# One state chain on one core: weight rows requested by ScalarE, stores and loads moved by half a pair, and the wide matrix work dealt out differently

## The chip, the core and the metric

The kernel runs on one core of one Trainium2 chip. The metric is the device time of one execution in microseconds (us). The engines are TensorE (PE; its weight loads are shown apart as PEld), VectorE (DVE), ScalarE (ACT), GpSimd (POOL) and SyncE (SP), which here only issues transfers. A letter q behind an engine (SPq, ACTq) means its queue of transfer requests, which is worked off in order: a request that has to wait for a semaphore holds up everything behind it on the same engine.

## The reference, cut to what matters

The reference is one layer of a decoder trunk on 1024 tokens of width 1024, in float32. The part around the change:

```
h = rms_norm(x);  z = h @ w_in            # pool, q, r/k/v + loras, 3 gates
y_pool = pool_branch(z_pool) @ w_proj_pool
y_mem  = mem_attention(z_q) @ w_proj_mem  # 4 heads, 256 memory tokens
# rwkv: 16 heads of 64, a state of 64x64 for each, step by step over the tokens
state = state * w_t + (state @ a_t) b_t^T + v_t k_t^T ;  y_t = state @ r_t
y_rwkv = (group_norm(y) + bonus) * g @ w_proj_rwkv
x = x + rms_norm((sum of the 3 gated branches) @ w_o);  then a ConvFFN
```

## The kernel before, in words

Every float32 weight row is split into a high and a low part, and each product of a wide matrix is made of three multiplications (high by high, high by low, low by high, lines 173 to 175). One weight block of the input projection (`in_block`, 128 output columns) has 8 k-steps for each of two halves of the tokens, so 16 k-steps or 48 multiplications of 128x512. Its weights come in four pieces of 128x256. For each piece `load_more` (line 159) requests the transfer into `wraw` on SP (line 163); `split_w` (line 129) then makes `whi` on ACT (line 131) and `wlo` on POOL (line 137). There are 3 buffers of `wraw` and 4 each of `whi` and `wlo`.

The state recurrence is done in chunks of 64 tokens. Four groups (`rwkv_group`, line 461, four heads each, g = 0 to 3) prepare it: gates and decays (`psu` products, line 488, then ACT), products of small matrices (`ps`, lines 586 and 593, and transposes `pt`, line 616), and a triangular solve that runs on DVE alone (31 steps, lines 639 and 641, then two transposes, lines 642 and 643). TensorE uses the solve's result in 32x32 products (`pz`, line 657, and `pw`, line 665). What a group made is spilled to memory.

Then one chain (`chain`, line 701) goes through 16 chunks, two to a pair. Each chunk is three visits of small products that depend on each other through copies on DVE and ACT: `pr`, then `py`/`pu` (with lines 764 and 773/774 behind them), then `ph`/`py` (with lines 790, 792 behind them). For each pair `load(b)` fetches `hv`, `ring`, `pair`, `bk` and `rb` (lines 718 to 722), one pair ahead. After a pair's second chunk `outputs` (line 680) loads two gate tiles `gt` (line 686), normalises the pair's output (a product `pvar`, line 693, and DVE operations, lines 695 to 698) and stores it as `d_y` (line 699).

Blocks that nobody waits for fill TensorE's time: 24 of the 32 blocks in the list `fill` (pool, query and gate columns, the results stored as `d_zp`, `d_zq`, `d_zg` by line 339) are dealt out by `fill_to(n)`, where n counts k-steps; the other 8 blocks stand in the attention that follows. `fill_to(n, behind)` makes the work wait in the scheduler's order behind a given instruction. Before the change n reaches 32, 48 and 64 behind the solves of groups 0, 1 and 2, then 96 and 160 in group 3; the chain asks for 172 at its first visit and 319 at its last, and the last 64 k-steps (to 384) stand behind the chain. The first thing behind them is the memory branch: loads of `mraw` (line 846), squares (line 850), a sum `pmm` (line 851), normalised halves `mh` and `ml`, and the key/value blocks. Its tiles lie in memory that the chain gives back.

The order on each engine is made by a scheduler from this program order, from data dependences, from buffer counts and from the extra order edges that `later` adds; those edges carry no semaphore.

Of the kernel before, what the change touches and what calls it, by code (L numbers as in the profile page):

```python
# [9 lines left out]
F32 = mybir.dt.float32  # L10
FR = mybir.dt.float32r
AF = mybir.ActivationFunctionType
ALU = mybir.AluOpType
# [4 lines left out]
P = 128  # L18
# [3 lines left out]
C = 64  # L22
# [22 lines left out]
def trunk_kernel(ctx: ExitStack, tc: tile.TileContext, xT, memT, pvec, w_in, w_kv, w_upd, w_upg,  # L45
                 w_pool, w_ppool, w_pmem, w_prwkv, w_o, w_fup, w_fdn, out):
    nc = tc.nc
    V, A, G, PE, SP = nc.vector, nc.scalar, nc.gpsimd, nc.tensor, nc.sync
# [15 lines left out]
    d_g = dtile([8, P, T], "d_g")  # L64
    d_bv = dtile([8, P, T], "d_bv")
# [4 lines left out]
    d_hv = dtile([NCH // 2, P, 4, 2, 2 * C], "d_hv")  # L70
    d_y = dtile([8, P, T], "d_y")
# [30 lines left out]
    for lo in (0, 64):  # L102
        s = slice(lo, lo + 64)
# [21 lines left out]
        return (lo_eng or V).tensor_tensor(lo, src, hi.bitcast(F32), op=ALU.subtract)  # L125

    hi_on_act, lo_on_dve, last_whi, hold = [False], [False], [None], [None]

    def split_w(src, hi, lo):
        if hi_on_act[0]:  # L130
            i = A.copy(hi, src)  # L131
            last_whi[0] = i.ins
            if hold[0] is not None:
                later(i, hold[0])
        else:
            G.tensor_scalar(hi, src, 1.0, 0.0, op0=ALU.mult, op1=ALU.add)
        (V if lo_on_dve[0] else G).tensor_tensor(lo, src, hi.bitcast(F32), op=ALU.subtract)  # L137
# [21 lines left out]
    def load_more(ps, ap, k0, n, kp):  # L159
        raw = wp.tile([P, kp, P], F32, name="wraw", tag=f"wraw{ps.c}", bufs=3)  # L160
        hi = wp.tile([P, kp, P], FR, name="whi", tag=f"whi{ps.c}", bufs=4)
        lo = wp.tile([P, kp, P], FR, name="wlo", tag=f"wlo{ps.c}", bufs=4)
        SP.dma_start(raw[:, :n], ap[:, k0:k0 + n])
        split_w(raw[:, :n], hi[:, :n], lo[:, :n])
        for j in range(n):
            ps.append((hi[:, j], lo[:, j]))
# [48 lines left out]
    def later(i, ins, plain=False):  # L215

        tc.add_manual_dep(i if plain else i.ins, ins.name, nosync, reason="order")
# [5 lines left out]
    rw = rw_ctx.enter_context(tc.tile_pool(name="rw", bufs=1))  # L223
# [7 lines left out]
    for k in range(KC):  # L231
        tag = ("X01", "X11", "HV", "HV")[k // 2]
# [228 lines left out]
    def rwkv_group(g, kv):  # L461
# [43 lines left out]
        for i in range(2):  # L505
            p = 2 * g + i
# [8 lines left out]
            for t0, _ in HALVES:  # L515
                s = slice(t0, t0 + 512)
# [124 lines left out]
            V.tensor_tensor(S[:, s + 1:, 0:m], S[:, s + 1:, 0:m], tm, op=ALU.add)  # L641
        V.transpose(S11.rearrange("p u s -> p s u"), S.rearrange("p t s -> p s t"))
        V.transpose(X.rearrange("p u t -> p t u"), S)
        if g == 3:
            fill_to(96)
        fill_to((32, 48, 64, 160)[g], solve if g == 3 else None)
        for us in (slice(0, NCH), slice(NCH, 2 * NCH)):
            for q, (qs, bs) in enumerate(quads):
                place = V.tensor_copy(NTu[qs, us, bs], X[qs, us]).ins
# [24 lines left out]
    def spill(dst, at_, src):  # L674
# [2 lines left out]
            dst = dst[:, :, n]  # L677
        SP.dma_start(dst.rearrange("c p t -> p c t"), src.rearrange("p (c u) s -> p c (u s)", u=2))

    def outputs(b, y, q):  # L680

        bt = slice(b * 2 * C, (b + 1) * 2 * C)
        gt = []
        for src, e in ((d_bv, "ld"), (d_g, "la")):
            gt.append(lr.tile([P, 8, 2 * C], F32, name="gt", tag=e))
            SP.dma_start(gt[-1], src[:, :, bt].rearrange("n p t -> p n t"))
        ln_w = pv[:, PV["ln_w"][0]:PV["ln_w"][0] + 8]
        for n in (0, 4):
            ns = slice(n, n + 4)
            y_, q_ = y[:, ns], q.rearrange("p (n t) -> p n t", t=2 * C)  # L690
            A.activation(q_, y_, AF.Square)
            ps = pss.tile([P, 512], F32, name="pvar", tag="s")
            PE.matmul(ps, bones, q, start=True, stop=True)
            rstd(q, ps, 2, 1.0 / 64)
            V.tensor_tensor(y_, y_, q_, op=ALU.mult)
            V.tensor_tensor(y_, y_, ln_w[:, ns].unsqueeze(2).broadcast_to([P, 4, 2 * C]), op=ALU.mult)
            V.tensor_tensor(y_, y_, gt[0][:, ns], op=ALU.add)
            V.tensor_tensor(y_, y_, gt[1][:, ns], op=ALU.mult)
        SP.dma_start(d_y[:, :, bt].rearrange("n p t -> p n t"), y)

    def chain(fills):

# [8 lines left out]
        def load(b):  # L711

            ar, nt = ring[:, b % 2], pair[:, b % 2, 0]
            hv = rw.tile([P, 8, 2, 2, C], F32, name="hv", tag=f"X{b % 2}2")
            rb = rw.tile([P, 8, 2, 2 * C], F32, name="rb", tag=f"X{b % 2}1")
            bk = rw.tile([P, 8, 2, P], F32, name="bk", tag=f"X{b % 2}0")
            for q, e in ((up, 0), (lo, 1)):
                SP.dma_start(hv[q, :, :, e], d_hv[b, q].rearrange("p g i (u s) -> p (g i) u s", u=2))
            SP.dma_start(ar, d_ar[b].rearrange("p g i e t -> p (g i) e t"))
            SP.dma_start(nt, d_nt[b].rearrange("p g i t -> p (g i) t"))  # L720
            SP.dma_start(bk, d_bk[b].rearrange("p g i u s -> p (g i) u s"))
            SP.dma_start(rb, d_rb[b].rearrange("p g i e t -> p (g i) e t"))
            held[b] = ar, nt, hv, rb, bk, pair[:, b % 2, 1]
# [25 lines left out]
        for c in range(NCH):  # L749
            b, u = divmod(c, 2)  # L750
            if u == 0 and 0 < b < NCH // 2 - 1:
                load(b + 1)
            ar, nt, hv, rb, bk, y = held[b]
            t = slice(u * C, (u + 1) * C)
            once = dict(start=True, stop=True)
            pr = bank("pr")
            py = pss.tile([P, 8, C], F32, name="py", tag="s")
            ke, ko = (up, lo) if c == 0 else (slice(0, P), slice(0, P))
            row = []
            for i in range(8):  # L760
                row.append(((pr[up, i], ar[ko, i, 2, t], hv[ko, i, u, 1]), once))
                row.append(((pr[lo, i], ar[ke, i, 0, t], hv[ke, i, u, 0]), once))
            visit(row, ready)
            made = V.tensor_copy(Rs, pr).ins
            pu = bank("pu")
            row = []
            for i in range(8 if c else 0):
                kw = dict(start=i == 0, stop=False)
                row.append(((py[lo, i], hv[lo, i, u, 0], ar[lo, i, 1, t]), kw))
                row.append(((py[up, i], hv[up, i, u, 1], ar[up, i, 1, t]), kw))  # L770
            row += [((pu[q, i], nt[q, i, t], Rs[q, i]), once) for i in range(8) for q in (lo, up)]
            visit(row, made)
            V.tensor_copy(hv[lo, :, u, 0], pu[lo])
            ready = A.copy(hv[up, :, u, 1], pu[up]).ins
            row = []
            if c + 1 < NCH:
                ph = bank("ph")
                for i in range(8):
                    row.append(((ph[up, i], bk[:, i, u, 64:128], hv[:, i, u, 1]), once))
                    row.append(((ph[lo, i], bk[:, i, u, 0:64], hv[:, i, u, 0]), once))  # L780
            for i in range(8):
                kw = dict(start=c == 0 and i == 0, stop=i == 7)
                row.append(((py[lo, i], hv[:, i, u, 0], rb[:, i, 0, t]), kw))
                row.append(((py[up, i], hv[:, i, u, 1], rb[:, i, 1, t]), kw))
            visit(row, ready)
            if c + 1 < NCH:
                hx = held[(c + 1) // 2][2]
                for q, e in ((lo, 0), (up, 1)):
                    if c == 0:
                        ready = V.tensor_copy(hx[q, :, 1 - u, e], ph[q]).ins  # L790
                    else:
                        ready = V.tensor_tensor(hx[q, :, 1 - u, e], ph[q], Hd[q], op=ALU.add).ins
                if c + 2 < NCH:
                    if c == 0:
                        V.tensor_copy(Hn, ph)
                    else:
                        V.tensor_tensor(Hn, ph, Hd, op=ALU.add)
                    for i in range(8):
                        A.activation(Hd[:, i], Hn[:, i], AF.Identity, scale=Dc[:, i, c + 1:c + 2])
            A.copy(y[:, :, t], py)  # L800
            if u:
                outputs(b, y, root)

    fill = [(j, spilled(d_zp[j])) for j in range(4)] + [(4 + j, spilled(d_zq[j])) for j in range(4)]
    fill += [(34 + j, spilled(d_zg[j], col("gate_b", j))) for j in range(24)]
# [2 lines left out]
    def fill_to(n, behind=None):  # L808

        while len(filled) < n:  # L810
            j, ev = fill.pop(0)
            in_block(j, ev, 1, filled, behind)
        return filled[n - 1]
# [6 lines left out]
    hi_on_act[0] = True  # L820
    for g in range(4):
        kv = rwkv_group(g, kv)
    chain(lambda v: 172 + 148 * v // 47)
    fill_to(384)
    rw_ctx.close()
    lr_ctx.close()

# [945 lines left out]
```

## Time and profile before

| | |
|---|---|
| median of 3 runs | 2033.92 us (2033.43 to 2038.42) |
| the profiled execution, its own time | 2039.66 us |
| its span, first to last instruction | 2037.9 us |
| mean granted TensorE clock | 0.976 |
| solves and `pz` products of groups 0 to 3 | `pz` starts at 226.3, 360.2, 508.1 and 643.2 us |
| chain | first `pr` at 672.4 us, last `pvar` at 907.9 us |
| memory branch and attention | first `pmm` at 944.1 us, last `po` at 1089.7 us |

Rows of groups read: line, engine, operation, out<-in, shape, count, busy time, mean ns of one, idle time before them and what ended it. A row of the timeline reads: start, duration, engine, line, operation, out<-in, count, and in brackets how long the engine had been idle before it and what released it. A row of waits reads: who waited for whom, total us, times, longest us. A row of windows reads: the stretch, its length, then busy time and count of PE, PEld, DVE, ACT and POOL, the mean granted TensorE clock (1.00 is full), the busy share of the transfer engines and GB/s.

### The profile page before, as it was taken

Reading aid. Unit: us, or ns where it says so; the run is one execution under the profiler, and the core shown is the slowest. Engines: PE = TensorE matmul, PEld = TensorE weight load, DVE = VectorE, ACT = ScalarE, POOL = GpSimd, SP = SyncE. Lnnn points to the kernel's source line nnn. Section 1 sums busy time; section 2 is a strip of 40 time slices with the busy share of each in tenths; the row PEclk is TensorE's granted clock in tenths of the full one; section 3 lists DMA queues with packets and bytes.
Section 4 is the critical chain, followed back from the end, with each engine's and each line's share of the span. In section 5 each row is a group of like instructions: output and inputs, shape, how many; then the busy total and the mean of one; then the engine's idle time right before and its main releaser. Section 6 shows DMA issues by size and latency. Waiting matters only on the chain.

```text
span 2037.9 us, 33739 instructions
## 1 busy us (share of the span) xinstructions
PE 1950.6 (96%) x12218; PEld 1574.1 (77%) x12218; DVE 1346.7 (66%) x2015; ACT 1048.9 (51%) x2158; POOL 779.2 (38%) x867
## 2 busy tenths in 40 slices
PE   7999998998988989899999999999999999999997
PEld 5777776776777767678788888887878888888886
DVE  8677669649664234443763453668889888877698
ACT  6675574753752334444555334546545544545544
POOL 4422213203201110112222345555579888832441
PEclk9999999979988999999999999999999999999999
DMA  4325244243276679845324544545322222269776
GB/s 153 127 80 164 84 141 123 71 130 101 85 223 218 203 237 263 226 139 173 105 81 158 189 134 128 181 146 174 109 91 88 78 88 83 83 214 244 166 184 148
DMA packets 284998, 296.25 MB, mean 145 GB/s; under 512 B 34720, under 2 KB 235552, under 8 KB 281760
## 3 DMA queue, kind: packets, MB, share of 16 engines
q1 hardware_dynamic: 271904, 278.90, 44.6%
q0 software_dynamic: 11856, 14.16, 4.3%
q8 instruction: 96, 1.57, 0.3%
q10 hardware_dynamic: 1072, 1.05, 0.2%
q14 instruction: 70, 0.57, 0.1%
HBM read 207.00 MB, written 87.03 MB: 144 GB/s over the span
## 4 chain that ended last, share of the span: by engine, by line
PE 49%; DVE 1%; DMA 1%; issue 0%; ACT 0%; POOL 0%; SPq 0%; ACTq 0%; DVEq 0%; POOLq 0%
PE psg L175 7%; PE psg L173 7%; PE psg L174 7%; PE psf L175 5%; PE psf L173 5%; PE psf L174 5%; PE psd L174 3%; PE psd L175 3%; PE psd L173 3%; PE ptr L964 0%; DMA d_f<-ug 0%; PE psn L1239 0%; PE po L173 0%; DMA wraw<-in_w_fup 0%; DMA kvr<-in_w_kv 0%
## 5 line engine op out<-in xcount | busy, mean ns | idle before, releaser
L137 POOL TENSOR_TENSOR wlo<-wraw,whi 128x256 fp32r<-128x256 f32 x464 | 398.1, 870 | 961.6 <-ACT whi L131 912.4
L173 PE MATMUL psg<-hh,whi 128*128 128x512 f32 x928 | 379.4, 409 | 32.2 <-ACT whi L131 25.6
L175 PE MATMUL psg<-hh,wlo 128*128 128x512 f32 x928 | 372.7, 402 | 2.6 <-POOL wlo L137 2.4
L174 PE MATMUL psg<-hl,whi 128*128 128x512 f32 x928 | 374.5, 404 | 0.7 <-DVE hl L259 0.6
L131 ACT CAST whi<-wraw 128x256 fp32r<-128x256 f32 x472 | 180.8, 403 | 245.7 <-PE psg L174 89.9
L173 PEld LDWEIGHTS psg<-hh,whi 128*128 128x128 f32 x928 | 178.2, 192 | 76.9 <-ACT whi L131 27.5
L175 PEld LDWEIGHTS psg<-hh,wlo 128*128 128x128 f32 x928 | 177.8, 192 | 44.8 <-POOL wlo L137 6.9
L174 PEld LDWEIGHTS psg<-hl,whi 128*128 128x128 f32 x928 | 178.3, 192 | 40.6 <-issue 2.5
L1099 POOL TENSOR_TENSOR wt<-a,wt 128x256 fp32r<-128x256 f32 x136 | 156.6, 1175 | 36.2 <-ACT wt L1098 36.1
L174 PE MATMUL psd<-f,u 128*128 128x512 f32 x292 | 113.8, 390 | 0.2 <-DVE f L1515 0.2
L175 PE MATMUL psd<-f,u 128*128 128x512 f32 x292 | 113.7, 389 | 0.0
L173 PE MATMUL psd<-f,u 128*128 128x512 f32 x292 | 113.2, 391 | 0.0
L175 PE MATMUL psf<-h2h,wt 128*128 128x512 f32 x272 | 106.0, 390 | 0.9 <-POOL wt L1099 0.9
L173 PE MATMUL psf<-h2h,wt 128*128 128x512 f32 x272 | 106.0, 390 | 0.3 <-ACT wt L1098 0.3
L174 PE MATMUL psf<-h2l,wt 128*128 128x512 f32 x272 | 105.9, 389 | 0.0
L1113 DVE SCALAR_TENSOR_TENSOR d<-z,pv,d 128x1023 f32<-128x1023 f32 x68 | 100.4, 1479 | 2.3
L1099 POOL TENSOR_TENSOR wt<-s,wt 128x256 fp32r<-128x256 f32 x68 | 79.6, 1190 | 3.7 <-ACT wt L1098 2.9
L173 PE MATMUL psf<-t,wt 128*128 128x512 f32 x204 | 79.4, 389 | 0.0
L175 PE MATMUL psf<-t,wt 128*128 128x512 f32 x204 | 79.4, 389 | 0.0
L174 PE MATMUL psf<-t,wt 128*128 128x512 f32 x204 | 79.4, 389 | 0.0
L1111 ACT ACTIVATE d<-z,pv 128x1024 f32<-128x1024 f32 x34 | 42.4, 1247 | 66.2 <-DVE z L1193 50.5
L1098 ACT CAST wt<-a 128x256 fp32r<-128x256 f32 x136 | 50.7, 404 | 42.2 <-POOL wt L1099 23.4
(430 smaller groups left out, 4605.5 us busy)
## 6 DMA issues: line engine op xcount, KB each, us to landing
wraw<-in_w_in SPq DMA_DIRECT2D x232, 128.0 KB, 2.5
a<-in_w_fup SPq DMA_DIRECT2D x128, 128.0 KB, 2.4
d_ar<-AR SPq DMA_DIRECT2D x24, 512.0 KB, 3.4
ring<-d_ar SPq DMA_DIRECT2D x8, 1536.0 KB, 7.2
d_zg<-st SPq DMA_DIRECT2D x48, 256.0 KB, 2.8
wraw<-in_w_fup SPq DMA_DIRECT2D x80, 128.0 KB, 2.5
fraw<-d_f SPq DMA_DIRECT2D x33, 256.0 KB, 3.9
d_rb<-RB SPq DMA_DIRECT2D x16, 512.0 KB, 3.9
```

The costliest lines, as they stand in the source:

```text
L131: i = A.copy(hi, src)
L137: (V if lo_on_dve[0] else G).tensor_tensor(lo, src, hi.bitcast(F32), op=ALU.subtract)
L173: first = PE.matmul(ps, wh, xh, start=start, stop=False)
L174: PE.matmul(ps, wh, xl, start=False, stop=False)
L175: last_mm[0] = PE.matmul(ps, wl, xh, start=False, stop=stop).ins
L1098: A.copy(w[0][:, us], src[u])
L1099: low = eng.tensor_tensor(w[1][:, us], src[u], w[0][:, us].bitcast(F32), op=ALU.subtract)
L1111: A.activation(d, z, AF.Identity, scale=col("cw2", j), bias=col("cb", j))
L1113: V.scalar_tensor_tensor(d[:, n:], z[:, :T - n], col(cw, j), d[:, n:], op0=ALU.mult, op1=ALU.add)
```

## The change

Four things are changed; what is computed stays the same, and the instructions on each engine are the same in kind and number except that 48 requests for weight pieces go from SP to ACT and that the loads of `hv` have another shape.

1. From the solve of group 3 until the chain has ended, weight pieces are requested by ACT (`w_queue`). Each such request is ordered behind the ACT split two pieces earlier (`whis[-2]`).
2. The store of a pair's output and the loads of its gates leave `outputs`: `store(b - 1)` and `gate(b)` now stand after the first chunk of pair b, and the last store behind the chain.
3. `hv` is laid out with its two halves apart, so that a load writes one contiguous stretch per partition in place of 16 stretches of 64 numbers.
4. The fills reach 48, 96, 144 and 192 k-steps in groups 0 to 3 and 256 behind the solve of group 3; the chain asks for 262 at its first visit and 384 at its last, and nothing is left behind the chain.

```
+    w_queue, whis = [SP], []
...
+            whis.append(i.ins)
...
-        SP.dma_start(raw[:, :n], ap[:, k0:k0 + n])
+        ld_ = w_queue[0].dma_start(raw[:, :n], ap[:, k0:k0 + n])
+        if w_queue[0] is A:
+            later(ld_, whis[-2])
...
+        fill_to(48 * (g + 1))
         if g == 3:
-            fill_to(96)
-        fill_to((32, 48, 64, 160)[g], solve if g == 3 else None)
+            w_queue[0] = A
+            fill_to(256, solve)
...
+    def gate(b):
+        gates[b] = []
+        for src, e in ((d_bv, "ld"), (d_g, "la")):
+            gates[b].append(lr.tile([P, 8, 2 * C], F32, name="gt", tag=e))
+            SP.dma_start(gates[b][-1], src[:, :, b * 2 * C:(b + 1) * 2 * C].rearrange("n p t -> p n t"))
+    def store(b):
+        SP.dma_start(d_y[:, :, b * 2 * C:(b + 1) * 2 * C].rearrange("n p t -> p n t"), ready_y[b])
...
-            hv = rw.tile([P, 8, 2, 2, C], F32, name="hv", tag=f"X{b % 2}2")
+            hv = rw.tile([P, 2, 8, 2, C], F32, name="hv", tag=f"X{b % 2}2")
...
-                SP.dma_start(hv[q, :, :, e], d_hv[b, q].rearrange("p g i (u s) -> p (g i) u s", u=2))
+                SP.dma_start(hv[q, e], d_hv[b, q].rearrange("p g i (u s) -> p (g i) u s", u=2))
...
             A.copy(y[:, :, t], py)
-            if u:
+            if u == 0:
+                if b:
+                    store(b - 1)
+                gate(b)
+            else:
                 outputs(b, y, root)
+        store(b)
...
-    chain(lambda v: 172 + 148 * v // 47)
+    chain(lambda v: 262 + 122 * v // 47)
     fill_to(384)
+    w_queue[0] = SP
```

The order on SP in the middle of the chain, before: the rows run from the loads for the next pair over the store of the output to the weight pieces (`wraw`), the gate loads (`gt`) and the store of a fill's result (`d_zg`).

```order
L719 DMA ring<-d_ar 128x3072
L720 DMA pair<-d_nt 128x1024
L718 DMA hv<-d_hv 64x16x64 x2
L721 DMA bk<-d_bk 128x2048
L722 DMA rb<-d_rb 128x2048
L699 DMA d_y<-pair 128x8x128
L163 DMA wraw<-in_w_in 128x256 x3
L686 DMA gt<-d_bv 128x8x128
L163 DMA wraw<-in_w_in 128x256 x2
L686 DMA gt<-d_g 128x8x128
```

The same place on SP after the change.

```order
L732 DMA hv<-d_hv 64x1024 x2
L736 DMA rb<-d_rb 128x2048
L692 DMA gt<-d_bv 128x8x128
L696 DMA d_y<-pair 128x8x128
L692 DMA gt<-d_g 128x8x128
L343 DMA d_zg<-st 128x512
L733 DMA ring<-d_ar 128x3072
```

No weight piece stands behind the store of the output any more; what stands behind it is a gate load, the store of a fill's result and the loads for the next pair.

The order on ACT through one pair of the chain after the change: `whi` is the split of a weight piece, `wraw` the request of a later one, `hv` and `pair` copies of the chain, `Rs` the scaling of the state, `st` the copy of a fill's result out of PSUM.

```order
L813 ACTIVATE Rs<-Rs,Dc 128x64 x8
L132 CAST whi<-wraw 128x256
L165 DMA wraw<-in_w_in 128x256
L788 COPY hv<-pu 64x8x64
L132 CAST whi<-wraw 128x256
L165 DMA wraw<-in_w_in 128x256
L132 CAST whi<-wraw 128x256
L165 DMA wraw<-in_w_in 128x256
L132 CAST whi<-wraw 128x256
L342 ACTIVATE st<-psg,pv 128x512
L165 DMA wraw<-in_w_in 128x256
L814 COPY pair<-py 128x8x64
```

Before, ACT had the same splits and copies with no request between them, and the splits stood in runs of up to four. Now a request stands right behind a split, two splits ahead of the split that needs it, and one block falls to most pairs.

The order on TensorE at the end of group 1, before: wide multiplications (lines 173 to 175), then the first `psu` products of group 2, and after 13 more wide ones `pz`.

```order
L174 MATMUL psg<-hl,whi 128x512
L175 MATMUL psg<-hh,wlo 128x512
L488 MATMUL psu<-ld,uhi 128x512
L489 MATMUL psu<-ld,ulo_221 128x512
L488 MATMUL psu<-la,uhi 128x512
L489 MATMUL psu<-la,ulo_221 128x512
L173 MATMUL psg<-hh,whi 128x512
```

And after the change, at the same place.

```order
L178 MATMUL psg<-hl,whi 128x512
L179 MATMUL psg<-hh,wlo 128x512
L662 MATMUL pz<-tb_3272,NT 32x32 x32
L492 MATMUL psu<-ld,uhi 128x512
L493 MATMUL psu<-ld,ulo_221 128x512
L492 MATMUL psu<-la,uhi 128x512
L493 MATMUL psu<-la,ulo_221 128x512
```

The `psu` products have moved behind `pz`, and counted over the whole order the wide run ahead of them has grown from 140 multiplications to 236 in group 1, from 127 to 236 in group 2, from 212 to 260 in group 0 and from 192 to 239 in group 3; group 3's small products now have wide ones between them where before 58 small ones stood in a row. Between the chain's first `pr` and its last `pvar` the wide multiplications fall from 469 to 374, between the last `pvar` and the first `pmm` from 155 to 45, and from there to the last `po` of the attention from 311 to 228.

More of the change, by code (lines that the diff above doesn't have):

```diff
@@ L678, in spill @@
         SP.dma_start(dst.rearrange("c p t -> p c t"), src.rearrange("p (c u) s -> p c (u s)", u=2))
-    def outputs(b, y, q):
[L682 to L686, printed above, removed]
+    gates, ready_y = {}, {}
+    def gate(b):
[5 more added lines that the diff above has]
+        SP.dma_start(d_y[:, :, b * 2 * C:(b + 1) * 2 * C].rearrange("n p t -> p n t"), ready_y[b])
+    def outputs(b, y, q):
+        gt = gates[b]
         ln_w = pv[:, PV["ln_w"][0]:PV["ln_w"][0] + 8]
@@ L698, in outputs @@
             V.tensor_tensor(y_, y_, gt[1][:, ns], op=ALU.mult)
-        SP.dma_start(d_y[:, :, bt].rearrange("n p t -> p n t"), y)
+        ready_y[b] = y
     def chain(fills):
@@ L760, in chain @@
             for i in range(8):
-                row.append(((pr[up, i], ar[ko, i, 2, t], hv[ko, i, u, 1]), once))
-                row.append(((pr[lo, i], ar[ke, i, 0, t], hv[ke, i, u, 0]), once))
+                row.append(((pr[up, i], ar[ko, i, 2, t], hv[ko, 1, i, u]), once))
+                row.append(((pr[lo, i], ar[ke, i, 0, t], hv[ke, 0, i, u]), once))
             visit(row, ready)
@@ L768, in chain @@
                 kw = dict(start=i == 0, stop=False)
-                row.append(((py[lo, i], hv[lo, i, u, 0], ar[lo, i, 1, t]), kw))
-                row.append(((py[up, i], hv[up, i, u, 1], ar[up, i, 1, t]), kw))
+                row.append(((py[lo, i], hv[lo, 0, i, u], ar[lo, i, 1, t]), kw))
+                row.append(((py[up, i], hv[up, 1, i, u], ar[up, i, 1, t]), kw))
             row += [((pu[q, i], nt[q, i, t], Rs[q, i]), once) for i in range(8) for q in (lo, up)]
             visit(row, made)
-            V.tensor_copy(hv[lo, :, u, 0], pu[lo])
-            ready = A.copy(hv[up, :, u, 1], pu[up]).ins
+            V.tensor_copy(hv[lo, 0, :, u], pu[lo])
+            ready = A.copy(hv[up, 1, :, u], pu[up]).ins
             row = []
@@ L778, in chain @@
                 for i in range(8):
-                    row.append(((ph[up, i], bk[:, i, u, 64:128], hv[:, i, u, 1]), once))
-                    row.append(((ph[lo, i], bk[:, i, u, 0:64], hv[:, i, u, 0]), once))
+                    row.append(((ph[up, i], bk[:, i, u, 64:128], hv[:, 1, i, u]), once))
+                    row.append(((ph[lo, i], bk[:, i, u, 0:64], hv[:, 0, i, u]), once))
             for i in range(8):
                 kw = dict(start=c == 0 and i == 0, stop=i == 7)
-                row.append(((py[lo, i], hv[:, i, u, 0], rb[:, i, 0, t]), kw))
-                row.append(((py[up, i], hv[:, i, u, 1], rb[:, i, 1, t]), kw))
+                row.append(((py[lo, i], hv[:, 0, i, u], rb[:, i, 0, t]), kw))
+                row.append(((py[up, i], hv[:, 1, i, u], rb[:, i, 1, t]), kw))
             visit(row, ready)
@@ L789, in chain @@
                     if c == 0:
-                        ready = V.tensor_copy(hx[q, :, 1 - u, e], ph[q]).ins
+                        ready = V.tensor_copy(hx[q, e, :, 1 - u], ph[q]).ins
                     else:
-                        ready = V.tensor_tensor(hx[q, :, 1 - u, e], ph[q], Hd[q], op=ALU.add).ins
+                        ready = V.tensor_tensor(hx[q, e, :, 1 - u], ph[q], Hd[q], op=ALU.add).ins
                 if c + 2 < NCH:
```

## Prediction

> **What bounds the kernel now.** I read the page first, then TensorE's waits, then the timeline and the queue around the longest of them, then the granted clock just behind each.
>
> ```profile
> span 2037.9 us, 33739 instructions
> PE 1950.6 (96%) x12218; PEld 1574.1 (77%) x12218; DVE 1346.7 (66%) x2015; ACT 1048.9 (51%) x2158; POOL 779.2 (38%) x867
> ```
>
> TensorE is busy for 1950.6 of 2037.9 us, so all its idle time is 87 us. The change takes no work from it. What can be won is idle time, and time in which TensorE is busy at a lower clock. TensorE's waits between 340 us (the solve of group 1) and 960 us (just behind the chain):
>
> ```profile
> PE psg L173 <- ACT whi L131: 19.2, 3, 7.5
> PE psu L488 <- DVE tb L639: 9.2, 2, 4.9
> PE ps L593 <- DVE AR L589: 4.4, 3, 2.6
> PE ph L738 <- ACT hv L774: 2.1, 1, 2.1
> PE pt L616 <- ACT BKN L617: 2.0, 1, 2.0
> PE ps L586 <- DVE AR L596: 1.7, 3, 1.2
> PE pt L616 <- DVE BK L611: 1.2, 1, 1.2
> ```
>
> Three waits for a split weight cost 19.2 us, two for DVE in the middle of a solve 9.2 us. The longest, from SP's and TensorE's timelines and the waits of SP's queue in the same stretch:
>
> ```profile
> 726.82 0.43 SPq L722 DMA_DIRECT2D rb<-d_rb  x1
> 735.07 0.37 SPq L699 DMA_DIRECT2D d_y<-pair  x1
> 735.56 2.40 SPq L163 DMA_DIRECT2D wraw<-in_w_in  x3
> SPq L699 <- DVE pair L698: 7.8, 1, 7.8
> 740.25 0.80 PE L173 MATMUL psg<-hh,whi 128*128 128x512 f32 x1 [7.49 <-ACT whi L131]
> ```
>
> SP stood for 7.8 us in front of the output's store, which waited for DVE. The weight pieces stood behind it, were requested at 735.56, and TensorE idled 7.49 us until 740.25. The other two waits of this kind stand at the chain's start and two thirds through it. The granted clock behind the seven longest waits (a stretch each), and in an undisturbed stretch:
>
> ```profile
> 355.00:358.50 3.50, 3.38 (x9) 2.70 (x10) 3.43 (x4) 0.00 (x0) 0.00 (x0) 0.54 0.00 0
> 413.00:440.50 27.50, 27.50 (x149) 21.74 (x149) 10.66 (x20) 12.84 (x32) 0.00 (x0) 0.51 0.50 134
> 502.00:505.00 3.00, 3.00 (x8) 2.32 (x8) 3.00 (x2) 0.00 (x0) 0.00 (x0) 0.50 0.00 0
> 583.50:601.00 17.50, 14.27 (x63) 12.27 (x64) 11.37 (x18) 10.27 (x24) 0.00 (x0) 0.51 0.83 220
> 648.50:665.50 17.00, 14.17 (x209) 10.90 (x210) 0.70 (x1) 4.45 (x9) 2.82 (x4) 0.50 0.59 177
> 737.50:744.00 6.50, 3.75 (x9) 2.87 (x10) 0.00 (x0) 1.63 (x5) 2.16 (x4) 0.51 0.80 206
> 833.00:839.50 6.50, 3.24 (x8) 2.45 (x9) 0.00 (x0) 0.78 (x2) 1.42 (x2) 0.50 1.05 305
> 1100.00:1150.00 50.00, 50.00 (x222) 41.44 (x221) 17.07 (x21) 25.77 (x48) 16.12 (x19) 1.00 0.75 247
> ```
>
> Each long wait is paid twice: behind it the clock is halved for 3 to 27 us, in which TensorE was busy for 69 us in all. A wide multiplication takes 50/222 = 0.225 us at full clock and 3.38/9 = 0.376 us in the first of these stretches, a loss of 40%.
>
> **The change part by part: gains.**
>
> *Weight pieces on ACT, stores and gates moved.* In the new order no weight piece stands behind the store of the output, so the wait on SP holds up only gates, fill stores and loads for the next pair. I take all three waits as gone: 19.2 us. The `ph` wait of 2.1 us goes too: it stands at a visit that had no wide work in front of it, and the new visits have 7 to 20 wide multiplications there. Their half-clock stretches (14.17, 3.75 and 3.24 us busy) give 40% of 21.2 = 8.5 us.
>
> *More wide work behind the solves.* Where 140 wide multiplications stood ahead of `psu` in group 1, 236 now stand ahead of `pz` and `psu` behind that; in group 2 it is 236 in place of 127. 96 more take 96 x 0.225 = 21.6 us, over four times the wait of 4.9 us. The 9.2 us go, and with them the stretches at 355 and 502 (6.4 us busy, 40% is 2.6 us).
>
> *Small products of groups 2 and 3.* The same place in group 1:
>
> ```profile
> 277.07 0.90 PE L593 MATMUL ps<-AR,BK 64*128 64x128 f32 x6 [0.97 <-DVE AR L589]
> ```
>
> The `ps` and `pt` waits add to 4.4 + 2.0 + 1.7 + 1.2 = 9.3 us. Group 3 gets wide work between its small products, and groups 2 and 3 now follow a solve as group 1 did, which waited 0.97 us there. I take half, 4.6 us. The stretches at 413 and 583.5 are 41.8 us busy; 40% is 16.7 us; small products may lose less, and one stretch may come back elsewhere: I take 10 us, between 0 and 16.7.
>
> Gains: 19.2 + 2.1 + 8.5 + 9.2 + 2.6 + 4.6 + 10 = 56.2 us.
>
> [...] The second and fourth stretches follow these waits:
>
> ```profile
> 412.76 0.47 PE L593 MATMUL ps<-AR,BK 64*128 64x128 f32 x1 [2.64 <-DVE AR L589]
> 582.07 1.15 PE L616 MATMUL pt<-ident,BK 128*128 128x128 f32 x8 [2.02 <-ACT BKN L617]
> ```
>
> Waits of 2.64 and 2.02 us are followed by 27 and 17 us at half clock, so I count the removal of waits of 2 us as removing stretches. [...]
>
> **Part by part: costs.**
>
> *The hole behind the chain.* This is what the 64 k-steps behind the chain covered. The last `pvar`, the output's store, the first load of the memory branch, its first square, and what DVE did meanwhile:
>
> ```profile
> 907.92 1.11 PE L693 MATMUL pvar<-Rs,bonesr 128*128 128x512 f32 x2
> 914.19 0.38 SPq L699 DMA_DIRECT2D d_y<-pair  x1
> 919.65 0.81 SPq L846 DMA_DIRECT2D mraw<-in_memT  x2
> 921.79 0.42 ACT L850 ACTIVATE msq<-mraw 128x256 f32<-128x256 f32 x1 [3.16 <-DMA mraw<-in_memT]
> 949.97 1.28 DVE L858 SCALAR_TENSOR_TENSOR mraw<-mraw,pv,mrs 128x256 f32<-128x256 f32 x3 [35.81 <-ACT mrs L207]
> ```
>
> The loads of `mraw` take memory that the chain gives back, and go out when the last store has landed: 13.9 us from `pvar` to the first square. Before, 155 wide multiplications (35 us) stood there; now 45, or 10.1 us, and with `pvar` about 10.7. TensorE idles 3.2 us, then some 2 us more while the other seven rows come in (0.4 us apart on SP). With 40% of a 3.4 us stretch: 6.5 us. If the 45 were late too, it would be 13.9 + 5 = 19 us; if other wide work is drawn in, 2 us.
>
> *Requests on ACT.* No request on ACT stands in the chain before; the nearest rows are ACT's three at the kernel's end, SP's own for weights in the chain, with their time to landing (min, median, max), two neighbouring splits, and ACT's load in the chain:
>
> ```profile
> L1686 ACTq DMA_DIRECT2D out_T<-acc x3: 378/381/425, 2032.3 to 2034.3; - x3
> L163 SPq DMA_DIRECT2D wraw<-in_w_in x40: 327/330/3730, 669.5 to 894.0; - x40
> DMA to landing us min/median/max: 2.3/3.0/7.8
> 929.12 0.41 ACT L131 CAST whi<-wraw 128x256 fp32r<-128x256 f32 x1 [0.44 <-PE psg L174]
> 930.48 0.41 ACT L131 CAST whi<-wraw 128x256 fp32r<-128x256 f32 x1 [0.95 <-PE psg L174]
> 672.00:908.00 236.00, 217.84 (x2998) 170.53 (x2997) 93.69 (x134) 103.60 (x249) 29.64 (x39) 0.97 0.76 217
> ```
>
> 48 requests at 0.381 us are 18.3 us on an engine busy 103.6 of 236 us. That alone is hidden. What isn't sure to be hidden is the lead: a request goes out two splits ahead, or 2 x 1.36 = 2.7 us when the splits run at TensorE's pace, and lands after 3.0 us (2.3 to 7.8). So ACT waits 0.3 us or more for the third and fourth piece of a block, in front of the chain's copies. TensorE has up to a block in hand and is not stopped by the weights themselves. Bounds: 0 (all covered) and 12 blocks x 1.5 us = 18 us; I take 6, nearer the median landing.
>
> *Contention.* Rows from the transfers between 640 and 920 us:
>
> ```profile
> DMA packets 53678, 60.11 MB, mean 215 GB/s; under 512 B 14576, under 2 KB 46704, under 8 KB 50928
> hv<-d_hv SPq DMA_DIRECT2D x12, 256.0 KB, 7.3
> ```
>
> The chain shrinks by 95 wide multiplications (21 us) and its waits, so the same loads come faster. The engines are busy 76% of the chain; 236 x 0.76 = 179 us of transfers in some 195 us, less what the longer rows of `hv` save (14576 short packets are mostly its). Loads go out a pair ahead, so I price this at 0, at most 10 us. At the chain's start 33 wide multiplications at full clock cover the round trip of `d_nt` where 38 at half clock did: 1 us.
>
> *Attention.* It loses 83 wide multiplications (18.7 us). In its stretch:
>
> ```profile
> 950.00:1090.00 140.00, 135.10 (x784) 114.83 (x783) 101.22 (x198) 77.35 (x200) 27.41 (x32) 0.99 0.32 104
> ```
>
> DVE's 101 us now have to fit into 121 us, 84%. Still under, but with dependent steps: 4 us, between 0 and 10.
>
> Costs: 6.5 + 6 + 0 + 1 + 4 = 17.5 us. Net gain 56.2 - 17.5 = 38.7 us. The profiled execution took 2039.66 us by its own time, 5.7 us over the median 2033.92. 2039.7 - 38.7 - 5.7 = 1995.3; I say 1996.
>
> **The rivals.**
>
> *ACT takes SP's place (slower).* ACT works in order, so a late weight piece now blocks the chain's own copies as well. If each of the 12 blocks stops TensorE as SP's waits did (19.2 / 3 = 6.4 us and 40% of some 4 us), that is 12 x 8 = 96 us in place of 6: 1996 + 90 = 2086 us. It decides from 3.7 us per block on, where the net gain is gone. For it: landings up to 7.8 us under load. Against: the median of 3.0, and the block in hand. Chance 0.06.
>
> *The covers are used up (smaller gain).* The hole is 19 us, the attention loses 10, ACT 12, and the two product stretches stay: 1996 + 12.5 + 6 + 6 + 10 = 2030 if all come together, 2012 to 2020 if half do. For it: 155 wide multiplications become 45 and DVE stood idle 35.81 us there. Chance 0.2.
>
> *The transfers are the limit, not the queue.* If the late weights came from full transfer engines, another queue brings nothing: the 19.2 and 8.5 us stay, 1996 + 27.7 = 2024 us. [...] Against the rival stands the row of 735.07: 7.8 us passed before the request, 2.4 us in making three. Chance 0.08.
>
> *Nothing moves.* The order shows all parts moved; waits would have to reappear in kind. 2034 us, chance 0.04.
>
> **How the numbers follow.** Forecast 0.62 (own range 1978 to 2010). The range 1977 to 2021 takes in the bounds of the gains (6.7 us more in the product stretches, 4.7 more waits, 6 less on ACT) and most of the second rival. A measurement can tell about 0.3%, 6 us, from no change: faster is under 2027.8. Forecast, most of the second rival and the third lie there: 0.9; same 0.05; slower 0.05.
>
> **What would show it.** Right: no TensorE wait for `whi` over 2 us between 640 and 900; no SP weight request behind `d_y`; no `psu` wait on a solve; at most two half-clock stretches from 340 us to the end of the chain; a wait of 3 to 6 us at `pmm`. Wrong: ACT idle on `wraw` in front of `hv` or `pair` copies, with TensorE waiting on lines 774 or 800; a wait at `pmm` over 10 us; half clock through the small products in spite of no wait.

## The result, and the profile after

The changed kernel takes 2013.48 us (median of 4 runs, 2008.79 to 2020.54) against 2034.55 us for the kernel before in the same session (4 runs, 2033.43 to 2038.42). The ratio is 0.9896, 95% interval 0.9857 to 0.9935: 21 us less, where 38.7 were forecast from the profiled execution. The profiled execution after took 2018.09 us by its own time. Its page:

```profile
span 2016.4 us, 33782 instructions
PE 1940.6 (96%) x12218; PEld 1556.6 (77%) x12218; DVE 1351.4 (67%) x2015; ACT 1047.2 (52%) x2158; POOL 789.0 (39%) x867
```

TensorE still idles for 76 us of the span (87 before). TensorE's longest waits between 340 and 960 us (engine, line, what is waited for: us in total, times, longest) say that it idles at other places:

```profile
PE pvar L707 <- ACT Rs L705: 16.8, 6, 4.1
PE psg L177 <- ACT whi L132: 7.8, 4, 4.3
PE ps L597 <- DVE AR L593: 2.5, 2, 1.7
PE pmm L871 <- ACT msq L870: 1.3, 1, 1.3
```

The waits of `psu` on a solve are gone. So are the long waits on `whi` inside the chain; the four that are left lie between 629 and 668 us, behind the last solve, where the first of the three waits before stood (6.0 us, up to 651.3). The hole behind the chain is the 1.3 us of `pmm`. What is new is the first row: `pvar`, the product that normalises a pair's output, waits once in each of six pairs for `Rs`, which ACT makes from `pair`. ACT's timeline ahead of the longest of them, with its requests (ACTq) among its work, and TensorE's row:

```profile
746.59 0.41 ACT L132 CAST whi<-wraw 128x256 fp32r<-128x256 f32 x1 [0.37 <-PE psg L178]
746.65 0.33 ACTq L165 DMA_DIRECT2D wraw<-in_w_in  x1
753.78 0.40 ACT L132 CAST whi<-wraw 128x256 fp32r<-128x256 f32 x1 [6.79 <-DMA wraw<-in_w_in]
753.86 0.33 ACTq L165 DMA_DIRECT2D wraw<-in_w_in  x1
754.94 0.40 ACT L132 CAST whi<-wraw 128x256 fp32r<-128x256 f32 x1 [0.76 <-DMA wraw<-in_w_in]
755.96 0.58 ACT L814 COPY pair<-py 128x512 f32<-128x512 f32 x1
756.57 0.63 ACT L705 ACTIVATE Rs<-pair 128x512 f32<-128x512 f32 x1
757.25 2.07 PE L707 MATMUL pvar<-Rs,bonesr 128*128 128x512 f32 x2 [4.06 <-ACT Rs L705]
```

ACT stands for 6.79 us in front of a cast whose weight piece has not landed: the piece was asked for at 745.26 us, behind the cast two before it, and landed 8.4 us later. Behind the late cast stand one more, the copy of `py` and the square `Rs`; TensorE has used up its block by then and waits 4.06 us. All weight pieces between 690 and 900 us, requests and time to landing, and the stretches behind two of the waits (the column behind the engines is the granted clock):

```profile
L165 ACTq DMA_DIRECT2D wraw<-in_w_in x26: 334/334/924, 700.1 to 870.8; - x26
DMA to landing us min/median/max: 2.3/4.5/10.6
```

```profile
757.50:764.00 6.50, 6.50 (x19) 4.08 (x20) 3.46 (x5) 3.56 (x10) 0.00 (x0) 0.56 1.02 234
788.50:794.50 6.00, 6.00 (x18) 3.62 (x18) 3.46 (x5) 3.38 (x9) 0.00 (x0) 0.54 0.99 252
```

A piece lands after 4.5 us (median), and a request goes out two casts ahead, 2.7 us by the prediction's rows. Five of the six waits are followed by half clock. In the trace's record of the granted clock the half-clock stretches between 200 and 1900 us add up to 88.7 us before and 41.0 after.

Where the time went, by stage. The marks are the first and the last `py` product of the chain, from the row that groups all 512 of them:

```profile
L738 PE MATMUL py<-rb,hv x512: 221/222/271, 687.5 to 901.9; 128*64 128x64 f32 x171
```

```profile
L752 PE MATMUL py<-rb,hv x512: 222/222/270, 710.9 to 921.0; 128*64 128x64 f32 x171
```

Counted over the order on TensorE, 253 wide multiplications moved to ahead of the first `py`, 58 out of the chain and 195 out of what follows; at 0.225 us they are 57, 13 and 44 us. So the stage ahead of the chain, 23.4 us longer, gained 33.5 us; the chain, 4.3 us shorter, lost 8.7; the rest, 40.6 us shorter (1136.0 to 1095.4), lost 3.3. Together that is 21.5, the difference of the spans. The forecast by the same stages was +37.1 (all of the gains but the two later `whi` waits with their half clock and the `ph` wait, less 1), +12.1 (those, less 6 for the requests) and -10.5. What is missing is missing in the chain.

### The profile page after: what moved, and what is told of

Same layout as the page of the kernel before. It is cut to its first block, busy times and chain, and to the rows that moved or that the text cites. A ratio compares the mean times of both kernels' runs of the same rounds, so it can differ in the third digit from the quotient of the medians.

```text
span 2016.4 us, 33782 instructions
## 1 busy us (share of the span) xinstructions
PE 1940.6 (96%) x12218; PEld 1556.6 (77%) x12218; DVE 1351.4 (67%) x2015; ACT 1047.2 (52%) x2158; POOL 789.0 (39%) x867
## 3 DMA queue, kind: packets, MB, share of 16 engines
q8 instruction: 96, 1.57, 0.3%
## 4 chain that ended last, share of the span: by engine, by line
PE 70%; DVE 11%; DMA 10%; ACT 5%; issue 3%; POOL 1%; SPq 0%; ACTq 0%; POOLq 0%; DVEq 0%
PE psg L177 12%; PE psg L179 12%; PE psg L178 12%; PE psf L179 5%; PE psf L177 5%; PE psf L178 5%; DMA wraw<-in_w_in 5%; PE psd L178 3%; PE psd L179 3%; PE psd L177 3%; DVE tb L643 1%; PE py L752 1%; DMA g<-d_zg 1%; DVE tb L645 1%; PE ps L597 1%
## 5 line engine op out<-in xcount | busy, mean ns | idle before, releaser
L139 POOL TENSOR_TENSOR wlo<-wraw,whi 128x256 fp32r<-128x256 f32 x464 | 407.5, 892 | 905.5 <-ACT whi L132 855.1
L177 PE MATMUL psg<-hh,whi 128*128 128x512 f32 x928 | 378.4, 408 | 21.6 <-ACT whi L132 13.9
```

The costliest lines, as they stand in the source:

```text
L177: first = PE.matmul(ps, wh, xh, start=start, stop=False)
```

## Experiments

Theory A: ACT's requests are too short ahead. A late piece stops ACT in its order, and the pair's copies behind it stop TensorE. Rival B: the transfers are the limit, and another lead or queue changes nothing. Rival C: other waits of the same size stand behind. All times are medians; a ratio is to the kernel before, with its 95% interval.

### A longer lead on ACT (e1_lead5)

```diff
-        raw = wp.tile([P, kp, P], F32, name="wraw", tag=f"wraw{ps.c}", bufs=3)
+        tag, bufs = f"wraw{ps.c}", 3
+        if w_queue[0] is A:
+            turn5[0] = (turn5[0] + 1) % 5
+            if turn5[0] > 2:
+                tag, bufs = "uhi", 2
+        raw = wp.tile([P, kp, P], F32, name="wraw", tag=tag, bufs=bufs)
-            later(ld_, whis[-2])
+            later(ld_, whis[-4])
```

> Edit: the changed kernel, with two more raw weight buffers while ScalarE sends the requests, so that a piece is asked for four casts ahead instead of two. Theory A (the lead is too short: a weight piece lands late, ScalarE stands in front of its cast, and the copies of the pair behind it in ScalarE's order come late): the six waits of pvar on ScalarE (16.8 us) and the waits on whi (7.8 us) shrink to under 4 us together, and the half-clock stretches behind them (six from 757 on, about 37 us, which cost half of that) go; 1975 to 1990 us. Rival B (the transfers themselves are the limit: the DMA engines are full when the next pair is loaded): the pieces land as late as before, the waits move by less than 5 us in all; 2008 to 2015 us. Rival C (a longer lead uncovers another wait of the same size): 1995 to 2008 us, with a new row among TensorE's waits.

Measured: 1976.67 us, ratio 0.9726 (0.9706 to 0.9745). TensorE's longest waits between 340 and 960 us, all pieces between 690 and 900 us, and the stretch of the chain:

```profile
PE ps L602 <- DVE AR L598: 2.6, 2, 1.7
PE pu L757 <- DMA pair<-d_nt: 2.1, 1, 2.1
PE psg L182 <- ACT whi L132: 2.1, 2, 1.7
PE pmm L876 <- ACT msq L875: 1.4, 1, 1.4
```

```profile
L170 ACTq DMA_DIRECT2D wraw<-in_w_in x21: 334/334/839, 690.9 to 811.7; - x21
DMA to landing us min/median/max: 2.3/6.0/12.7
```

```profile
640.00:905.00 265.00, 260.24 (x3423) 1.00 0.75 234
```

The pieces land later than in the changed kernel (median 6.0 us against 4.5), and yet one `pvar` wait of 0.4 us is all that is left and the clock is 1.00 there (0.93 in the changed kernel). In the traces TensorE works in the same order in both kernels up to 870 us, a stretch that has five of the six waits, so it was not a change of its order that removed them. Theory A holds: it was the lead, not the speed of the transfers. B and C fall.

### Requests back on SP (e1_sp_queue) and five buffers there (e2_sp_lead5)

The first undoes one line of the change; the second adds to it the two buffers of above, used from the last solve to the end of the chain.

```diff
         if g == 3:
-            w_queue[0] = A
             fill_to(256, solve)
```

```diff
+        if turn5[0] is not None:
+            turn5[0] = (turn5[0] + 1) % 5
+            if turn5[0] > 2:
+                tag, bufs = "uhi", 2
```

> Edit: the changed kernel with all weight requests left on SP, as in the kernel before; the shifted store and gate loads and the new dealing stay. If the move of the queue was what removed the three waits of about 6 us behind the store of y: these waits come back, 15 to 25 us more than the changed kernel, 2028 to 2038 us. If the shift of the store was enough, and ScalarE's requests cost more than they brought: no wait on whi over 2 us, no pvar waits on ScalarE, 1985 to 2005 us.

> Edit: the changed kernel with the weight requests on SP and five raw buffers instead of three in the same stretch. Theory: on SP a request goes out as soon as its buffer is free, three pieces ahead, and that is enough: within 5 us of three buffers (1981.2), 1976 to 1984 us. Rival: the last waits there (whi 2.2 us, ph on ScalarE 3.1 us) are late pieces too: 1968 to 1975 us.

Measured: 1981.16 us, 0.9739 (0.9723 to 0.9755), and 1974.48 us, 0.9708 (0.9685 to 0.9731). TensorE's longest waits in the first, same stretch as above, and its marks:

```profile
PE ph L751 <- ACT hv L787: 3.1, 3, 1.4
PE ps L597 <- DVE AR L593: 2.5, 2, 1.6
PE psg L177 <- ACT whi L132: 2.2, 3, 1.7
PE pu L751 <- DMA pair<-d_nt: 1.4, 1, 1.4
```

```profile
L751 PE MATMUL py<-rb,hv x512: 222/222/270, 701.7 to 886.3; 128*64 128x64 f32 x171
```

The waits did not come back on SP, as the second theory had it, and the time is under both ranges. Two more buffers there bring some 7 us more, into the rival's range, and the `ph` waits are gone; but the intervals just overlap, so the lead on SP stays undecided. One line of the change, the move to ACT, cost 32 us: the chain takes 184.6 us with the requests on SP and 210.1 with them on ACT. Half clock falls from 41.0 to 3.4 us. With early requests the engine that asks makes no difference that shows (1976.67 on ACT, 1974.48 on SP, intervals overlap). What decided here is what stands behind a late piece in the asking engine's own order.

### The parts alone (e1_deal_only, e2_shift_only, e3_hv_only)

The kernel before with the new `fill_to` numbers; with the shifted stores and gate loads and the new layout of `hv`; with the layout alone. The edits, one after the other:

```diff
-        if g == 3:
-            fill_to(96)
-        fill_to((32, 48, 64, 160)[g], solve if g == 3 else None)
+        fill_to(48 * (g + 1))
+        if g == 3:
+            fill_to(256, solve)
-    chain(lambda v: 172 + 148 * v // 47)
+    chain(lambda v: 262 + 122 * v // 47)
```

```diff
-            if u:
+            if u == 0:
+                if b:
+                    store(b - 1)
+                gate(b)
+            else:
                 outputs(b, y, root)
```

```diff
-            hv = rw.tile([P, 8, 2, 2, C], F32, name="hv", tag=f"X{b % 2}2")
+            hv = rw.tile([P, 2, 8, 2, C], F32, name="hv", tag=f"X{b % 2}2")
-                SP.dma_start(hv[q, :, :, e], d_hv[b, q].rearrange("p g i (u s) -> p (g i) u s", u=2))
+                SP.dma_start(hv[q, e], d_hv[b, q].rearrange("p g i (u s) -> p (g i) u s", u=2))
```

> Edit: the kernel before with the new dealing of the fill blocks alone; requests, stores and gate loads as they were. Theory: the waits of psu on the solve (9.2 us), half of the ps and pt waits, their half clock and the half-clock stretches of the product phases go, the three waits on whi behind the store of y stay: 15 to 26 us less than before, 2008 to 2019 us. Rival: what the product phases gain is taken from the chain, which now has fewer fill steps to stand in, or the stalled requests meet more blocks: 2028 to 2040 us.

> Edit: the kernel before with the shifted stores and gate loads and the new layout of hv alone; weight requests on SP and the dealing as before. Theory: the three waits on whi behind the store of y (19.2 us), the wait of ph (2.1 us) and their half clock (8.5 us) go, everything else stays: 30 us less than before, 1998 to 2010 us. With the new dealing alone (16.7 us less) that makes 47 of the 52 us that both together brought without ScalarE's queue. Rival: the shift only pays when the fill blocks are dealt anew as well: 2015 to 2030 us.

> Edit: the kernel before with the new layout of hv alone. Theory L (the layout carries a good part of what the shift seemed to bring, since the old layout cost 23 us where the weight requests stood on SP behind the new dealing): 2010 to 2024 us, and of the three waits on whi at least one goes. Rival (weight pieces are held by the store of y on SP, and how the hv loads are cut matters only once that is gone): 2029 to 2038 us, waits on whi as before.

Measured: the dealing 2016.53 us, 0.9923 (0.9906 to 0.9939); shift with layout 2016.46, 0.9910 (0.9890 to 0.9930); layout alone 2016.85, 0.9914 (0.9899 to 0.9928). The dealing lies in the range of its theory, but not in its way (below). Shift with layout lies in its rival's range, and the layout alone does all that the two do together, in the range of theory L. TensorE's longest waits in it, its SP's wait for DVE between 640 and 905 us, and some of SP's requests through one pair:

```profile
PE psu L488 <- DVE tb L639: 9.5, 2, 5.0
PE ps L593 <- DVE AR L589: 4.5, 3, 2.6
PE pw L665 <- ACT tb L660: 4.0, 1, 4.0
PE psg L173 <- ACT whi L131: 3.6, 3, 1.7
```

```profile
SPq L699 <- DVE pair L698: 29.3, 8, 9.6
```

```profile
702.03 2.79 SPq L163 DMA_DIRECT2D wraw<-in_w_in  x3
707.35 0.33 SPq L719 DMA_DIRECT2D ring<-d_ar  x1
714.06 0.43 SPq L722 DMA_DIRECT2D rb<-d_rb  x1
724.60 0.37 SPq L699 DMA_DIRECT2D d_y<-pair  x1
725.06 1.69 SPq L163 DMA_DIRECT2D wraw<-in_w_in  x2
```

SP still waits up to 9.6 us for DVE ahead of the store, and weight pieces still stand behind it. But the waits on `whi` have shrunk from 19.2 to 3.6 us. So the store alone was not what made them.

Nor did it stand ahead of all three. The first wait before ends at 651.3 us, and the first store goes out at 709.7. Its three pieces were asked for behind `rb`, `ring` and `bk`, the chain's first loads:

```profile
L163 SPq DMA_DIRECT2D wraw<-in_w_in x3: 395/428/436, 639.1 to 640.1; - x3
DMA to landing us min/median/max: 11.5/11.6/11.7
```

At the second wait `rb`, asked for at 726.82, landed 10.0 us later, and the pieces, asked for from 735.56, landed from 739.7. At the third `rb` and the pieces both went out behind the store and landed 7.2 and 5.7 us later. In all three the pieces landed 1 to 3 us behind a large load of the chain.

The layout changes two things. The first is the order that the scheduler makes. Before, SP asks for no piece between the gate loads (712.71 us) and the store (735.07); with the layout alone three go out at 702.03, ahead of the loads for the next pair. The second is the packets: those under 512 bytes between 690 and 880 us fall from 13832 to 1649, and SP is held for less time in making its requests. The longest one for `rb` takes 3.6 to 7.8 us in the six kernels of this case with the old layout and 0.7 to 1.7 us in the eight with the new one. But the longest before, 7.3 us at 765.77, is followed by no wait of TensorE on `whi`; at its three waits `rb` took 0.3, 0.4 and 2.0 us. What part of the 16 us is the order and what part the packets is not shown.

In the dealing alone, the `psu` waits go, but the chain gets worse. Its waits:

```profile
PE psg L173 <- ACT whi L131: 17.6, 5, 12.4
PE pvar L693 <- ACT Rs L691: 10.8, 4, 3.5
PE ph L738 <- ACT hv L774: 4.5, 4, 1.4
```

Its marks are 704.0 and 925.9 us: ahead of the chain it gains 57 - 16.5 = 40.5 us, and in the chain, which 61 wide multiplications (13.7 us) left, it loses 7.5 + 13.7 = 21.2. There is less wide work to stand behind, and the pieces still come late. So its theory missed twice, a larger gain and a loss that its rival had named, and the time came out in its range by luck. It fits that the dealing (16 us, by its ratio) and shift with layout (18) bring 53 together: with both, the chain no longer loses.

### The layout undone (e2_old_hv, e3_sp_lead5_old_hv, e3_after_old_hv)

The old layout put back with the requests on SP, the same with five buffers, and in the changed kernel (each with its other lines on `hv`):

```diff
-            hv = rw.tile([P, 2, 8, 2, C], F32, name="hv", tag=f"X{b % 2}2")
+            hv = rw.tile([P, 8, 2, 2, C], F32, name="hv", tag=f"X{b % 2}2")
```

> Edit: the changed kernel with the weight requests on SP and the old layout of hv, so that its loads go in packets under 512 bytes again. Theory: the transfers are not what the chain waits for, so the number of packets costs nothing: 1977 to 1986 us, as with the new layout (1981.2). Rival: the short packets hold up the loads of each next pair and the weight pieces among them: 1988 to 2000 us, with waits on whi or on hv.

> Edit: the weight requests on SP, five raw buffers, and the old layout of hv. Theory: the short packets only make pieces late, and the longer lead covers that: within 6 us of the new layout (1974.5), 1970 to 1982 us. Rival: the old layout costs time of its own, in VectorE's and ScalarE's steps on hv or in the loads of hv: 1988 to 2000 us.

> Edit: the changed kernel with the old layout of hv alone. Theory: short packets make the weight pieces later, and with a lead of two casts ScalarE waits for each: 8 to 25 us more than the changed kernel, 2020 to 2036 us, with longer waits of pvar or whi. Rival: ScalarE's late requests set the pace already, and the layout adds nothing: 2008 to 2018 us.

Measured: 2004.04 us, 0.9849 (0.9825 to 0.9872), so 23 us for the layout; 1991.61, 0.9789 (0.9772 to 0.9807), so 17 us, and the longer lead does not cover it; 2007.29, 0.9863 (0.9844 to 0.9882), no difference from the changed kernel that the intervals allow. My theory was wrong in all three; the first lies 4 us above its rival's range, the second in it, the third 1 us under it. In the first, waits of `whi` are back; the second view has SP's requests at one pair's end, two rows with the new layout (e1_sp_queue) and two with the old:

```profile
PE psg L177 <- ACT whi L132: 14.8, 5, 6.4
PE pvar L706 <- ACT Rs L704: 5.3, 2, 3.0
PE ph L751 <- ACT hv L787: 3.8, 3, 2.1
```

```profile
768.53 2.88 SPq L165 DMA_DIRECT2D wraw<-in_w_in  x3
778.61 0.38 SPq L695 DMA_DIRECT2D d_y<-pair  x1
779.50 0.37 SPq L695 DMA_DIRECT2D d_y<-pair  x1
781.96 3.52 SPq L165 DMA_DIRECT2D wraw<-in_w_in  x3
```

Here too the order changes with the layout: the three pieces go out 10 us ahead of the store with the new one and behind it with the old. So the 23 and 17 us are the price of the layout together with the order that comes with it. The steps on `hv` are not the cause: DVE's copy takes 0.68 us and ACT's 0.58 with either layout. With five buffers SP is still held: `rb` takes 7.8 us at 718 us, where TensorE does not wait, and `gt` 5.1 us at 806, just ahead of four weight requests, and TensorE waits 6.5 us for `whi` up to 817.

The changed kernel is the one place where the order hardly changes: TensorE's is the same up to 906 us. There 13793 short packets in place of 1513 cost nothing. The weight pieces do not pass through SP in it. That ACT's late pieces then set the pace with either layout agrees with the 12.3 us of `pvar` waits with the old one, but is only argued.

### The shift undone (e1_old_store, e2_lead5_old_store), and the lead alone (e3_before_lead5)

Store and gate loads put back to the end of each pair, in the changed kernel and with the long lead on ACT; and the kernel before with the five buffers of above and nothing else:

```diff
-            if u == 0:
-                if b:
-                    store(b - 1)
-                gate(b)
-            else:
+            if u:
                 outputs(b, y, root)
```

> Edit: the changed kernel with the store of y and the gate loads put back to the end of each pair; weight requests stay on ScalarE. Theory: with the weight requests off SP nothing urgent stands behind that store, so the time stays within 4 us of the changed kernel's, 2009 to 2018 us. Rival: the gate loads come late and VectorE's output steps, or the loads of the pair after next, wait for SP: 10 to 20 us more, 2023 to 2034 us.

> Edit: the changed kernel with five raw buffers and requests four casts ahead on ScalarE, and the store of y and the gate loads back at the end of each pair. Theory: the shift and the other queue are two answers to the same wait; where the requests are early and off SP, the shift adds nothing: 1972 to 1982 us, as with the shift (1976.7). Rival: the loads of the next pair but one, behind the store on SP, come late: a wait for ring, hv or gates of 2 us and more in each pair, 1985 to 2000 us.

> Edit: the kernel before with five raw buffers instead of three from the last solve to the end of the chain, nothing else. Theory: the lead is what counts, wherever it comes from; two more pieces in hand are two more casts of about 1.3 us each to be covered, so each of the three waits on whi of about 6.4 us shrinks by 2.6 us, with part of its half clock: 2016 to 2028 us. Rival 1 (they vanish, as the store only just delays the pieces): 2000 to 2012 us. Rival 2 (SP is stuck as long as before and more pieces only wait behind it together): 2030 to 2038 us.

Measured: 2010.21 us, 0.9890 (0.9876 to 0.9905); 1979.44, 0.9728 (0.9706 to 0.9751); 2027.22, 0.9965 (0.9950 to 0.9979). Where the pieces do not stand behind the store, the shift is worth nothing that shows; in the first of these TensorE's order is that of the changed kernel throughout. With the new dealing, requests on SP and the old layout, it brought 12 to 15 us (2016.53 to 2004.04 us, 0.9923 to 0.9849). Not tried: the shift undone with the requests on SP and the new layout. The lead alone is worth 6 us to the kernel before. That lies in the range of its theory, but not in its way: the waits on `whi` fall from 19.2 to 12.1 us, and one of them is 10.1 us, longer than any before.

The kernel with requests on SP and five buffers, 1974.48 us, is faster than both kernels compared here, by 59 us (0.9708) than the one before.

## Why the prediction was right and wrong

**The sign and the range were right; the size was half.** The step that failed is "Requests on ACT", priced at 6 with an upper bound of 18. It measured 32.3 us (2013.48 - 1981.16). By the two pages TensorE idles 20.3 us more with the requests on ACT (2016.4 - 1940.6 against 1980.7 - 1925.2) and is busy 15.4 us longer with the same products: 35.7, the difference of the spans. Most of the idle time is the 16.8 us of `pvar` waits and 7.8 - 2.2 = 5.6 more on `whi`; the longer busy time goes with 41.0 - 3.4 = 37.6 us more at half clock. Two things were mis-sized. The lead of 2.7 us was set against a landing of 3.0 us, the median of SP's pieces over the whole chain; on ACT the pieces landed after 4.5 us by median and 10.6 at worst. And the price counted ACT's wait, with TensorE's block in hand as cover, but not the half clock behind it.

That the time fell into the range is in part luck: ACT's requests cost 26 us more than priced, past their bound, and the stage behind the chain 7 us less. The time lies outside the forecast's own range (1978 to 2010) and in the 2012 to 2020 us of half of the second rival, whose hole and attention did not come. The signs say the same: ACT idle on `wraw` in front of the `pair` copy was a sign of being wrong, and seven half-clock stretches stand between 340 us and the chain's end where two were allowed.

**ACT takes SP's place** was the right mechanism at chance 0.06. At 32 us over 12 blocks it cost 2.7 us a block, under the 3.7 from which the sign would have turned.

**Weight pieces, stores and gates moved.** Two of the three waits went; in place of the first, 6.0 us, the changed kernel has 7.8 us between 629 and 668 us. The row of the store was read as the cause of all three because SP stood 7.8 us in front of it at one of them. The first has no store ahead of it, and with the layout alone SP stands at the store as long while the waits on `whi` shrink to 3.6 us. The prediction passed over the loads of the next pair, just behind which the pieces landed.

**Contention, priced at 0,** held the largest part that I had not seen: the layout of `hv`, with the order that comes with it, is worth 16 us alone and 23 beside the new dealing on SP. I gave it no gain of its own. The rival "the transfers are the limit" was right that the queue's move did not help, and the pieces did land late behind the chain's loads. But that is not a limit as such: with a longer lead they landed later still (6.0 us against 4.5 by median), and 0.4 us of the `pvar` waits was left.

**More wide work, small products, half clock.** The `psu` and `pt` waits went, and with them the products' half clock except one stretch of 3.4 us. For the stage ahead of the chain 37.1 us were forecast; it gained 33.5 in the changed kernel, 40.5 with the dealing alone and 57 - 14.2 = 42.8 with the requests on SP. This part was right; that the changed kernel is 4 to 9 us short of the others fits its requests again, with the waits on `whi` from 629 to 668 us. The price of half clock was a little low: wide products there start 0.427 us apart (356.11, 356.54 and 356.96 in TensorE's timeline before), against 0.227 at full clock, a loss of 47% and not 40; the 3.38/9 counted products that the window cuts.

**The hole behind the chain** was 1.3 us, not 6.5, and the waits in the attention stayed at 1.9 us or less each row; together that stage lost 3.3 us where 10.5 were priced. The first square came 12.1 us behind the last `pvar` (13.9 before). The 45 wide multiplications there were not late, as their pieces had been asked for ahead of the last store.

**Waits of 2 us.** The prediction counted the removal of the waits of 2.64 and 2.02 us as removing the stretches behind them. These waits went, and the stretches of 27.3 and 17.1 us with them; what half clock the changed kernel has between 340 and 640 us is one stretch of 3.41 us from 582.36 us on, behind a `ps` wait of 1.67 us. That not every wait of 2 us is followed by half clock is shown at the end.

## What to carry to other kernels

Before a request moves to another engine's queue, read what stands behind the instruction that will wait for its landing, and set the lead against the slowest landing in that stretch, not the median. A wait in front of one row of a queue does not make that row the cause: look at every wait of the kind, and at what lands just ahead of the late piece. Where a scheduler makes the order, a new layout can move requests too: compare the orders before the layout is named as the cause. And moving filler work from a stage to an earlier one costs the stage that it leaves its cover, so it pays fully only once that stage's own late transfers are cured.

## What the runs showed of the hardware

In the traces' record of the granted clock the half-clock stretches of one execution start on a grid of 3.413 us (in the changed kernel four of them start 30.72 us, nine steps, apart from each other) and between 340 and 905 us last whole steps of it (in the kernel before 3.41, 27.31, 3.41, 17.07, 17.07, 6.83 and 6.83 us). I laid TensorE's gaps, from the traces of all fourteen kernels between 200 and 960 us, on that grid. All 54 steps at full clock with more than 1.81 us idle were followed by half clock in the next step. Of the 18 with 1.58 to 1.81 us 11 were, and of the 58 with 1.0 to 1.57 us one. In the two kernels compared here it is all 14 with 1.66 us or more, seven in each, and none of the 10 with 1.0 to 1.57. (Ends of products are modelled in the profile.) So in these traces the half clock goes with the idle time within one step, not with the length of the wait; a sharp bound between 1.58 and 1.81 us is not shown. These three rows are a wait of 2.00 us in the changed kernel, one of 2.14 us with the long lead on ACT, cut by the grid into parts of at most 1.21 us, and one of 1.59 us with the requests on SP, each with the stretch behind it:

```profile
882.40 0.93 PE L707 MATMUL pvar<-Rs,bonesr 128*128 128x512 f32 x1 [2.00 <-ACT Rs L705]
882.70:886.10 3.40, 3.40 (x39) 1.98 (x38) 0.49 (x1) 1.32 (x2) 0.00 (x0) 0.50 0.92 375
```

```profile
695.58 1.15 PE L757 MATMUL pu<-Rs,pair 64*64 64x64 f32 x32 [2.14 <-DMA pair<-d_nt]
697.80:701.20 3.40, 3.40 (x70) 2.52 (x69) 1.47 (x3) 0.85 (x2) 0.00 (x0) 1.00 0.02 5
```

```profile
579.21 0.90 PE L597 MATMUL ps<-AR,BK 64*128 64x128 f32 x6 [1.59 <-DVE AR L593]
580.20:583.50 3.30, 3.30 (x64) 3.28 (x62) 0.46 (x2) 2.84 (x6) 0.00 (x0) 0.50 0.81 226
```

The granted clock is 0.50, 1.00 and 0.50. In the third of these rows 1.59 us idle, some 47% of a step of 3.413 us, was followed by half clock.
